# Three query projections normalised in their exponentials, and the first four weight blocks loaded by pairs of input channels

## Chip, cores and metric

One core of one Trainium2 chip runs the kernel. The metric is the device time of one execution in microseconds; 1082.49 is the median of three runs of the kernel before. TensorE (PE in the profile) multiplies, VectorE (DVE) and ScalarE (ACT) do the elementwise work, GpSimd (POOL) a little of it, and SyncE (SP) issues most of the loads.

## The reference, cut to what matters

One decoder layer over 256 tokens of width 1024: a convolution branch and sparse attention share one input projection, then comes attention over a memory of 256 tokens, then a layer of 16,384 experts chosen by product keys (PEER).

```python
def rmsnorm(x, g):
    xf = x.astype(jnp.float32)
    y = xf * lax.rsqrt(jnp.mean(xf * xf, axis=-1, keepdims=True) + EPS)
    return (y * g.astype(jnp.float32)).astype(x.dtype)
...
        hn = rmsnorm(h, mix_norm_g[l])
        proj = hn @ w_in[l]
        conv_a, conv_b, q, k_c, v_c, k_s, v_s, k_w, v_w, gate_logits = jnp.split(proj, IN_SPLITS, axis=-1)
        y_conv = conformer_conv(conv_a, conv_b, conv_dw_w[l], conv_dw_b[l], conv_ln_g[l], conv_ln_b[l])
        y_nsa = nsa_mixer(q, k_c, v_c, k_s, v_s, k_w, v_w, gate_logits, positions,
                          cmp_pos[l], cmp_w1[l], cmp_b1[l], cmp_w2[l], cmp_b2[l])
        h = h + jnp.concatenate([y_conv, y_nsa], axis=-1) @ w_out[l]
        h = h + memory_attention(rmsnorm(h, mem_q_norm_g[l]), rmsnorm(mem, mem_kv_norm_g[l]),
                                 w_mem_q[l], w_mem_k[l], w_mem_v[l], w_mem_o[l])
        h = h + peer(rmsnorm(h, peer_norm_g[l]), peer_w_q[l], peer_sub_keys[l], peer_u[l], peer_v[l])
    return rmsnorm(h, final_norm_g)
```

The norm's factor is one number per token, so it can be multiplied in behind a projection. Where the projection gives queries, the factor scales a whole row of scores, and a positive factor changes neither the row's order nor the place of its maximum.

## The kernel before

All activations lie transposed: 128 channels on the partitions, 256 tokens along the free axis, 8 chunks of channels. A weight block is 128 x 1024 floats (512 KB). `wload` (line 124) brings one into one of four buffers named `raw`, from SP's queue. The input projection multiplies it as it is, eight matmuls of 256 columns into one accumulator (`proj1`, line 160). Later projections split it into a rounded part `hi` (ScalarE, line 141) and a remainder `lo` (VectorE, line 142; GpSimd for some), with three matmuls per chunk (`mm3`, lines 152 to 154).

TensorE's instructions run in the order in which the program writes them. On the other engines a scheduler sets the order when the kernel is built; each engine then works through its own list from first to last, so an instruction that waits holds up all behind it on its engine.

`Rstd` (line 197) makes the norm factors. `add` sums squares (`sa_`). `sums` (line 214) adds over the partitions with two tiny matmuls (`ss_`), and a chain of 12 small VectorE operations makes the factor per token as a column (`rsc_`, `.col`) and then two diagonal matrices (`dg_`). `rows` (line 229) spreads them with two matmuls (`sr_`) into a row over the tokens (`rs_`, `.row`), which ScalarE copies. The tags are x (the layer's input, `r0`), m (memory), c (convolution's norm, `rc`) and h, h2 (`r1`, `r2`; both print as h).

The program's course. TensorE begins with 14 passes over ones (`warm`, line 245). Lines 246 to 254 issue the first loads. `hx` is x times the gain. The loop at line 312 takes the convolution's eight weight blocks in pairs `pb`, `pa`: one block after the other, `r0.sums` behind the third, `r0.rows` in the middle of the fourth. `conv_in` (line 300) makes the gated input `u`, and 124 taps (line 298, `yc<-u`) follow on VectorE, handed out by `conv(n)` between other work and finished by `ln_mean` (sums `lsum`, lines 607 to 610) ahead of TensorE's `pmu` (line 616). Then come two blocks for keys and values, the rope's queries and keys (`pq`, in `qraw`), and the values. The memory's input `mT` (four loads of 256 KB) becomes `mg` and `mg_l`, and while the attention's chains run, TensorE is filled with the memory's keys and values (`pmk`, `pmv`). `scores` (line 548) takes 16 units: matmuls `pss`, maximum `amx`, exponential `ape`, sum `asm`. In `mq_out` (line 723) the memory's queries are multiplied with `r1.row` and split; `m_scores` follows. In the expert stage `pq_out` (line 829) multiplies with `r2.row`, `key_scores` (line 834) makes `psq`, copied out as `sco`, two blocks behind the projection. Then 16 rounds of top-k on VectorE choose experts while TensorE goes through the expert weights (`pu`, `Y`).

Of the kernel before, what the change touches and what calls it, by code (L numbers as in the profile page):

```python
# [89 lines left out]
def rope_constants():  # L90

    d = np.arange(P) % 64
    inv = (np.float32(500000.0) ** (-(np.arange(8, dtype=np.float32) * np.float32(2.0) / np.float32(16.0)))).astype(np.float32)
    return np.stack([np.where(d < 16, inv[d % 8], 0.0), np.where(d < 8, -1.0, np.where(d < 16, 1.0, 0.0))], axis=1).astype(np.float32)


def build(tc, A, out, dbg=None):
# [163 lines left out]


    posf = wk.tile([P, T], F32, name="posf", tag="tb")
    V.tensor_copy(posf, posi)
    ang = St = ch.tile([P, T], F32, name="St")
    V.tensor_scalar(ang, posf, Pm("inv"), None, op0=ALU.mult)
    kk = wk.tile([P, T], F32, name="kk", tag="ta")
    MAGIC = 12582912.0
    V.tensor_scalar(kk, ang, 1.0 / (2.0 * math.pi), MAGIC, op0=ALU.mult, op1=ALU.add)
    V.tensor_scalar(kk, kk, MAGIC, None, op0=ALU.subtract)  # L270
    c1 = 6.28125
    c2 = float((np.array([2.0 * math.pi - c1], np.float32).view(np.uint32) & np.uint32(0xFFFFF000)).view(np.float32)[0])
    c3 = 2.0 * math.pi - c1 - c2
    for c in (c1, c2, c3):
        V.scalar_tensor_tensor(ang, kk, -c, ang, op0=ALU.mult, op1=ALU.add)
    PIF = 3.1415925
    V.tensor_scalar(ang, ang, PIF, -PIF, op0=ALU.min, op1=ALU.max)
    aabs = Ct = ch.tile([P, T], F32, name="Ct")
    V.scalar_tensor_tensor(aabs, ang, -1.0, ang, op0=ALU.mult, op1=ALU.max)
    halfpi = cst.tile([P, 1], F32, name="halfpi")  # L280
    V.memset(halfpi, math.pi / 2)
# [29 lines left out]
    pend = []  # L311
    for i in range(4):
        pb = psum(T, f"pb{i}")
        wb = wload(A["w_in_t"][2 * i]) if i else w0
        proj1(pb, wb, hx)
        if i == 1:
            r0.sums()
        wa = wload(A["w_in_t"][2 * i + 1])
# [3 lines left out]
        proj1(pa, wa, hx, range(4))
        if i == 1:
            r0.rows()
            conv_in(*pend)
# [845 lines left out]
```

## Time and profile before

| | |
|---|---|
| median of three runs | 1082.49 us (1081.4 to 1082.73) |
| profiled execution, its own time | 1082.72 us |
| its span on the core | 1080.9 us |
| mean granted TensorE clock | 0.996 of full speed |
| TensorE busy | 1061.2 us, 98% |
| VectorE busy | 871.8 us, 81% |
| ScalarE busy | 580.0 us, 54% |
| GpSimd busy | 102.3 us, 9% |

Busy shares are means over the whole span. A wait counts only where TensorE, or a chain that it depends on, stands still for it. The profiled execution lies 0.23 us over the median.

### The profile page before, as it was taken

How to read it: one execution, taken by the hardware profiler on the slowest of the kernel's cores; microseconds unless marked ns; L12 is line 12 of the kernel's file. 1: busy time of each engine (PE TensorE's matmuls, PEld its weight loads, DVE VectorE, ACT ScalarE, POOL GpSimd, SP SyncE). 2: the span in 40 equal slices, each digit the busy share in tenths (PEclk: the TensorE clock that was granted, in tenths of full speed). 3: DMA queues.
4: the chain of work that ended last, by engine and by line, in shares of the span. 5: the costliest groups of instructions: out<-in, count | busy, mean ns of one | idle time of the engine just before them, and what ended most of it. 6: DMA issues, size and time to landing. Idle time of an engine off the chain costs nothing.

```text
span 1080.9 us, 20534 instructions
## 1 busy us (share of the span) xinstructions
PE 1061.2 (98%) x7346; PEld 976.3 (90%) x7346; DVE 871.8 (81%) x2226; ACT 580.0 (54%) x1334; POOL 102.3 (9%) x82
## 2 busy tenths in 40 slices
...
GB/s 245 247 127 151 98 99 117 196 98 174 159 116 178 178 193 167 160 162 157 162 164 163 163 150 160 156 203 201 194 190 193 194 192 192 195 194 193 195 195 78
DMA packets 51685, 182.45 MB, mean 169 GB/s; under 512 B 5760, under 2 KB 6528, under 8 KB 51456
## 3 DMA queue, kind: packets, MB, share of 16 engines
...
q14 instruction: 43, 0.35, 0.1%
HBM read 179.81 MB, written 1.05 MB: 167 GB/s over the span
## 4 chain that ended last, share of the span: by engine, by line
PE 85%; DVE 13%; ACT 1%; DMA 1%; issue 0%; SPq 0%; DVEq 0%; ACTq 0%
PE Y L1071 32%; PE pu L152 9%; PE pu L154 8%; PE pu L153 8%; PE pq L163 2%; PE pw L1017 1%; PE ppq L152 1%; PE ppq L153 1%; PE ppq L154 1%; PE pb L163 1%; PE pw L1018 1%; PE pa L163 1%; DVE ohx L948 1%; PE pmk L152 1%; DVE lo L142 1%; DVE ohx L946 1%
## 5 line engine op out<-in xcount | busy, mean ns | idle before, releaser
L141 ACT ACTIVATE hi<-raw 128x512 fp32r<-128x512 f32 x624 | 376.7, 626 | 176.7 <-PE pu L153 66.9
L142 DVE TENSOR_TENSOR lo<-raw,hi 128x512 fp32r<-128x512 f32 x556 | 369.1, 687 | 26.8 <-ACT hi L141 21.0
L152 PE MATMUL pu<-hn_h,hi 128*128 128x256 f32 x1024 | 296.3, 289 | 0.0
L154 PE MATMUL pu<-hn_h,lo 128*128 128x256 f32 x1024 | 290.7, 284 | 1.9 <-DVE lo L142 1.9
L153 PE MATMUL pu<-hn_l,hi 128*128 128x256 f32 x1024 | 290.7, 284 | 0.0
L154 PEld LDWEIGHTS pu<-hn_h,lo 128*128 128x128 f32 x1024 | 197.3, 193 | 2.1 <-DVE lo L142 2.1
L153 PEld LDWEIGHTS pu<-hn_l,hi 128*128 128x128 f32 x1024 | 197.4, 193 | 0.0
L152 PEld LDWEIGHTS pu<-hn_h,hi 128*128 128x128 f32 x1024 | 197.2, 193 | 0.0
L1071 PE MATMUL Y<-hi,al 128*128 128x512 f32 x512 | 158.3, 389 | 0.0
L1071 PE MATMUL Y<-lo,ah 128*128 128x512 f32 x512 | 158.3, 389 | 0.0
L1071 PE MATMUL Y<-hi,ah 128*128 128x512 f32 x512 | 158.2, 389 | 0.0
L1071 PEld LDWEIGHTS Y<-hi,al 128*128 128x128 f32 x512 | 96.1, 188 | 20.0
L1071 PEld LDWEIGHTS Y<-lo,ah 128*128 128x128 f32 x512 | 96.1, 188 | 19.9
L1071 PEld LDWEIGHTS Y<-hi,ah 128*128 128x128 f32 x512 | 96.1, 188 | 19.8
L167 DVE TENSOR_TENSOR al<-slB,ah 128x256 fp32r<-128x256 f32 x88 | 37.4, 425 | 86.1 <-PE Y L1071 86.1
L166 ACT ACTIVATE ah<-slB 128x256 fp32r<-128x256 f32 x88 | 36.8, 418 | 110.7 <-PE Y L1071 110.7
L142 POOL TENSOR_TENSOR lo<-raw,hi 128x512 fp32r<-128x512 f32 x68 | 94.8, 1421 | 11.8 <-ACT hi L141 9.2
L1023 ACT ACTIVATE slB<-pw 128x348 f32<-128x348 f32 (+31 forms) x64 | 32.5, 507 | 70.2 <-DVE slB L1022 57.0
L298 DVE SCALAR_TENSOR_TENSOR yc<-u,par,yc 128x256 f32<-128x256 f32 x120 | 54.8, 474 | 0.1
L167 DVE TENSOR_TENSOR al<-slA,ah 128x256 fp32r<-128x256 f32 x40 | 17.1, 428 | 37.3 <-PE Y L1071 37.3
L166 ACT ACTIVATE ah<-slA 128x256 fp32r<-128x256 f32 x40 | 16.7, 418 | 49.3 <-PE Y L1071 48.0
L152 PE MATMUL ppq<-gx_h,hi 128*128 128x256 f32 x128 | 37.4, 292 | 0.0
...
## 6 DMA issues: line engine op xcount, KB each, us to landing
raw<-u SPq DMA_DIRECT2D x128, 512.0 KB, 3.4
raw<-v SPq DMA_DIRECT2D x128, 512.0 KB, 3.3
...
```

The source lines that it names most:

```text
L141: S.activation(hi, r, AF.Copy)
L142: (engs or (V, V))[q].tensor_sub(lo, r, hi.bitcast(F32))
L152: PE.matmul(ps, w[0], xh, start=start, stop=False)
L153: PE.matmul(ps, w[0], xl, start=False, stop=False)
L154: PE.matmul(ps, w[1], xh, start=False, stop=stop)
L163: PE.matmul(ps, w[0][:, k * P:(k + 1) * P], x[:, k], start=k == 0, stop=k == KC - 1)
L166: S.activation(dst[0], src, AF.Copy)
L167: V.tensor_sub(dst[1], src, dst[0].bitcast(F32))
L298: V.scalar_tensor_tensor(yc[:, i], u[:, i, j:j + T], w, yc[:, i], op0=ALU.mult, op1=ALU.add)
L946: V.tensor_tensor(o4, o4, tif[:, side].unsqueeze(2).to_broadcast([P, 16, 16, 8]), op=ALU.mult)
L1023: S.activation(slB[:, done - J:, n0:n0 + 4].rearrange("p i n -> p n i"), pw[:, :, done:], AF.Copy, scale=1.0 / GSC)
L1071: PE.matmul(Y[nh][c], lhs[:, sl], wc[c][t], start=False, stop=i == KEYS - 1 and lhs is a[1], skip_group_check=True)
```

## The change

Three parts. First, the start: the first four weight blocks come as 16 loads of 128 KB, by pairs of input channels, each quarter of all four blocks behind the other, on SP's queue; x and the first 32 columns of the parameters are issued from ScalarE's queue. TensorE works on all four blocks side by side, channel by channel. `r0.sums` stands behind all four, `r0.rows` behind the fifth block. The constants of the rope and the angles' operations come after the projections instead of ahead of them. Second, `qraw`, the memory's queries and the experts' queries are taken out of PSUM without the norm's factor, and the exponentials scale by the factor's column (`r8`, `r16`, `r2c`). `r1` makes no row and no diagonals any more. Third, the key scores follow one block behind the projection instead of two.

```diff
-        if cnt[0] == 1:
-            nc.sync.dma_start(raw[:, 0:512], src[:, 0:512])
-            nc.sync.dma_start(raw[:, 512:], src[:, 512:])
-        else:
-            nc.sync.dma_start(raw[:, 0:n], src)
+        nc.sync.dma_start(raw[:, 0:n], src)
...
-        def sums(self):
+        def sums(self, rows=True):
...
             rsqrt(y, m, t, sh)
+            if not rows:
+                return
...
-    nc.sync.dma_start(xT[:, 0:2], A["xT"][:, 0:2])
-    nc.sync.dma_start(par, A["par"])
-    w0 = wload(A["w_in_t"][0])
-    posi = wk.tile([P, T], I32, name="posi", tag="rt")
-    nc.sync.dma_start(posi, A["pos"].partition_broadcast(P))
-    for q in range(1, 4):
-        nc.sync.dma_start(xT[:, 2 * q:2 * q + 2], A["xT"][:, 2 * q:2 * q + 2])
+    nc.scalar.dma_start(par[:, 0:32], A["par"][:, 0:32])
+
+    first = [[wts.tile([P, 512], F32, name=f"wf{c}{h}", tag=("hi", "lo")[c // 2], bufs=6) for h in range(2)] for c in range(4)]
+    for q in range(4):
+        nc.scalar.dma_start(xT[:, 2 * q:2 * q + 2], A["xT"][:, 2 * q:2 * q + 2])
+        for c in range(4):
+            o = 256 * (q % 2)
+            nc.sync.dma_start(first[c][q // 2][:, o:o + 256], A["w_in_t"][c][:, 256 * q:256 * q + 256])
+    nc.sync.dma_start(con1, A["con"][:, 0:NCON1])
+    nc.sync.dma_start(par[:, 32:], A["par"][:, 32:])
...
+    acc = [psum(T, f"p{'ba'[c % 2]}{c // 2}", "mm" if c > 1 else "at") for c in range(4)]
+    for k in range(KC):
+        for c in range(4):
+            PE.matmul(acc[c], first[c][k // 4][:, (k % 4) * P:(k % 4 + 1) * P], hx[:, k], start=k == 0, stop=k == KC - 1)
+    r0.sums()
+    for i in range(2, 4):
+        pb = psum(T, f"pb{i}")
+        proj1(pb, wload(A["w_in_t"][2 * i]), hx)
+        if i == 2:
+            r0.rows()
+            conv_in(0, acc[0], acc[1])
+            conv_in(1, acc[2], acc[3])
+            conv(6)
+        pa = psum(T, f"pa{i}")
+        proj1(pa, wload(A["w_in_t"][2 * i + 1]), hx)
+        conv_in(i, pb, pa)
+        conv(6)
+    nc.sync.dma_start(con2, A["con"][:, NCON1:])
+    posi = wk.tile([P, T], I32, name="posi", tag="rt")
+    nc.sync.dma_start(posi, A["pos"].partition_broadcast(P))
...
-        V.tensor_mul(dst, ps, r0.row)
+        if i < 2:
+            V.tensor_mul(dst, ps, r0.row)
+        else:
+            S.activation(dst, ps, AF.Copy)
...
+    V.tensor_scalar(r8, r0.col, 0.125, None, op0=ALU.mult)
+    V.tensor_scalar(r8n, r0.col, -0.125, None, op0=ALU.mult)
...
-        V.tensor_scalar(mx, mx, -0.125, None, op0=ALU.mult)
+        V.tensor_scalar(mx, mx, r8n[:, hf:hf + 1], None, op0=ALU.mult)
...
-            S.activation(pe[:, b, 0:W], ps[:, b], AF.Exp, scale=0.125, bias=mx[:, b:b + 1], accum_out=sm[:, b:b + 1])
+            S.activation(pe[:, b, 0:W], ps[:, b], AF.Exp, scale=r8[:, hf:hf + 1], bias=mx[:, b:b + 1], accum_out=sm[:, b:b + 1])
...
-        t = twk.tile([P, T], F32, name=f"mqt{i}", tag="mqt", bufs=4)
-        V.tensor_mul(t, ps, r1.row)
-        S.activation(mq_h[:, i], t, AF.Copy)
-        V.tensor_sub(mq_l[:, i], t, mq_h[:, i].bitcast(F32))
+        split((mq_h[:, i], mq_l[:, i]), ps)
...
-    pq0 = mq_chunk(0)
-    r1.sums()
-    pq1 = mq_chunk(1)
-    pq2 = mq_chunk(2)
-    r1.rows()
-    mq_out(0, pq0)
-    mq_out(1, pq1)
-    mq_out(2, pq2)
-    for i in range(3, KC):
+    for i in range(KC):
         mq_out(i, mq_chunk(i))
+        if i == 1:
+            r1.sums(rows=False)
+            for j in range(2):
+                V.tensor_scalar(r16[j], r1.col, (0.0625, -0.0625)[j], None, op0=ALU.mult)
...
-        V.tensor_mul(qt, ps, r2.row)
+        S.activation(qt, ps, AF.Copy)
...
-        todo.append((i, ps))
-        if i == 0:
+        todo.append((i, pq_out(i, ps)))
+        if i == 1:
             r2.sums()
-        if i < 2:
-            continue
-        if i == 2:
+            V.tensor_copy(r2c, r2.col)
+        if i == 3:
             r2.rows()
-            todo = [(j, pq_out(j, p)) for j, p in todo]
-            continue
-        todo[-1] = (i, pq_out(i, ps))
-        key_scores(*todo.pop(0))
-        if i == 3:
+        if i:
             key_scores(*todo.pop(0))
...
-            tc.keep_in_program_order(S.activation(ge, ge, AF.Exp))
+            tc.keep_in_program_order(S.activation(ge, ge, AF.Exp, scale=r2c[:, hf:hf + 1]))
```

The change also moves rows on the other engines, which the diff does not show. VectorE at the end of the first norm's chain in the kernel before (`rsc_x` the factor, `dg_x` its diagonals, `mg_l` the remainders of the memory's input, `tb` and `ta` the gated convolution's input):

```order
L195 SCALAR_TENSOR_TENSOR rsc_x<-t_x,rsc_x 128x2
L227 TENSOR_SCALAR dg_x<-con_63,rsc_x 128x128 x2
L419 TENSOR_SCALAR chalf<-rsc_x 128x2
L239 SCALAR_TENSOR_TENSOR mg_l<-mT,par,mg 128x256 x2
L302 TENSOR_TENSOR tb_236<-pb_169,rs_x 128x256
L306 SCALAR_TENSOR_TENSOR ta_240<-pa_181,rs_x 128x256
```

And VectorE at the same place in the changed kernel:

```order
L233 SCALAR_TENSOR_TENSOR mg_l<-mT,par,mg 128x256
L185 TENSOR_TENSOR t_x<-rsc_x 128x2
L186 TENSOR_TENSOR t_x<-t_x,m_x 128x2
L233 SCALAR_TENSOR_TENSOR mg_l<-mT,par,mg 128x256
L187 SCALAR_TENSOR_TENSOR rsc_x<-t_x,rsc_x 128x2
L203 TENSOR_TENSOR sa_m<-sa_m,sq_m_414 128x256
L221 TENSOR_SCALAR dg_x<-con_63,rsc_x 128x128 x2
```

Two of the memory's remainders and one addition of its squares (`sa_m`) moved ahead of `dg_x`.

VectorE ahead of the thirteenth score maximum (`amx300`, whose reduction is the next row behind these) in the kernel before; `lo341` is the second remainder of a block of the memory's values, `yc` are taps:

```order
L142 TENSOR_TENSOR lo341_1695<-raw34_1688,hi341_1694 128x512
L298 SCALAR_TENSOR_TENSOR yc_168<-u_166,par_64,yc_168 128x256
L566 TENSOR_TENSOR asm210_1508<-asm210_1508,gate_652 128x2
L298 SCALAR_TENSOR_TENSOR yc_168<-u_166,par_64,yc_168 128x256
L167 TENSOR_TENSOR nsa_l_873<-po1_1540,nsa_h_872 128x256
L298 SCALAR_TENSOR_TENSOR yc_168<-u_166,par_64,yc_168 128x256
L559 TENSOR_REDUCE amx211_1569<-pss211_1563 128x2
L298 SCALAR_TENSOR_TENSOR yc_168<-u_166,par_64,yc_168 128x256
L560 TENSOR_SCALAR amx211_1569<-amx211_1569 128x2
L142 TENSOR_TENSOR lo350_1803<-raw35_1800,hi350_1802 128x512
L298 SCALAR_TENSOR_TENSOR yc_168<-u_166,par_64,yc_168 128x256 x2
L565 RECIPROCAL asm211_1573<-asm211_1573 128x2
```

VectorE from the thirteenth maximum in the changed kernel, where the same remainder is called `lo291`:

```order
L561 TENSOR_REDUCE amx300_1633<-pss300_1627 128x2
L274 SCALAR_TENSOR_TENSOR yc_174<-u_172,par_64,yc_174 128x256
L568 TENSOR_TENSOR asm211_1594<-asm211_1594,gate_669 128x2
L562 TENSOR_SCALAR amx300_1633<-amx300_1633,r81_673 128x2
L274 SCALAR_TENSOR_TENSOR yc_174<-u_172,par_64,yc_174 128x256
L573 TENSOR_SCALAR ape211_1593<-ape211_1593,asm211_1594 128x256
L274 SCALAR_TENSOR_TENSOR yc_174<-u_172,par_64,yc_174 128x256
L573 TENSOR_SCALAR ape211_1593<-ape211_1593,asm211_1594 128x256
L274 SCALAR_TENSOR_TENSOR yc_174<-u_172,par_64,yc_174 128x256
L567 RECIPROCAL asm300_1637<-asm300_1637 128x2
L134 TENSOR_TENSOR lo291_1655<-raw29_1648,hi291_1654 128x512
```

The remainder moved from ahead of that maximum to ten rows behind it, with four taps and two scaled exponentials between.

VectorE ahead of the convolution's sums in the kernel before (`lsum` is ready with the last row but one):

```order
L560 TENSOR_SCALAR amx301_1668<-amx301_1668 128x2
L142 TENSOR_TENSOR lo360_1867<-raw36_1864,hi360_1866 128x512
L609 TENSOR_TENSOR lsum2_1659<-yc_168 128x256
L142 TENSOR_TENSOR lo361_1871<-raw36_1864,hi361_1870 128x512
L610 TENSOR_TENSOR lsum_1657<-lsum_1657,lsum2_1659 128x256
L565 RECIPROCAL asm301_1672<-asm301_1672 128x2
```

And in the changed kernel, up to the row that completes `lsum`:

```order
L562 TENSOR_SCALAR amx301_1689<-amx301_1689,r81_673 128x2
L274 SCALAR_TENSOR_TENSOR yc_174<-u_172,par_64,yc_174 128x256
L134 TENSOR_TENSOR lo301_1716<-raw30_1709,hi301_1715 128x512
L274 SCALAR_TENSOR_TENSOR yc_174<-u_172,par_64,yc_174 128x256
L567 RECIPROCAL asm301_1693<-asm301_1693 128x2
L134 TENSOR_TENSOR lo310_1824<-raw31_1821,hi310_1823 128x512
L274 SCALAR_TENSOR_TENSOR yc_174<-u_172,par_64,yc_174 128x256
L568 TENSOR_TENSOR asm301_1693<-asm301_1693,gate_669 128x2
L134 TENSOR_TENSOR lo311_1828<-raw31_1821,hi311_1827 128x512
L611 TENSOR_TENSOR lsum2_1680<-yc_174 128x256
L573 TENSOR_SCALAR ape301_1692<-ape301_1692,asm301_1693 128x256
L612 TENSOR_TENSOR lsum_1678<-lsum_1678,lsum2_1680 128x256
```

Taps stand there up to four rows ahead of `lsum2`, and three remainders, a reciprocal and a scaled exponential are in the stretch, where two remainders were. Counted from the thirteenth maximum to the last sum, both rows included, there are 5 taps in the kernel before and 11 in the changed one.

## Rows read from the trace of the kernel before

**Rows 1.** Part 4 of the page: the chain that ended last, by engine.
```profile
PE 85%; DVE 13%; ACT 1%; DMA 1%; issue 0%; SPq 0%; DVEq 0%; ACTq 0%
```
**Rows 2.** Timeline, TensorE, first 31 us: start, length, instruction, idle before it and releaser.
```profile
1.03 6.03 PE L245 MATMUL warm<-ones 128*128 128x128 f32 x28 [1.03 <-DVE ones L242]
...
10.00 4.53 PE L163 MATMUL pb<-hx,raw 128*128 128x256 f32 x12 [2.07 <-DVE hx L259]
...
21.27 0.50 PE L218 MATMUL ss_x<-ones,sa_x 128*128 128x1 f32 x4
...
24.51 0.71 PE L233 MATMUL sr_x<-dg_x,ones 128*128 128x128 f32 x4 [0.90 <-DVE dg_x L227]
...
26.79 3.62 PE L163 MATMUL pb<-hx,raw 128*128 128x256 f32 x16
...
30.24 3.62 PE L163 MATMUL pa<-hx,raw 128*128 128x256 f32 x16
```
**Rows 3.** Waits of TensorE over the span: total us, times, longest us.
```profile
PE sr_c L233 <- DVE dg_c L227: 2.3, 1, 2.3
...
PE pu L154 <- DVE lo L142: 1.9, 1, 1.9
...
PE sr_h L233 <- DVE dg_h L227: 1.4, 1, 1.4
...
PE pmu L616 <- DVE asm L565: 1.1, 1, 1.1
```
**Rows 4.** Stretches: length, busy time by engine, granted clock, DMA share, GB/s.
```profile
core 0: us, PE busy (x) PEld busy (x) DVE busy (x) ACT busy (x) POOL busy (x), PEclk, DMA share, GB/s
...
2.00:13.00 11.00, 8.93 (x37) 7.94 (x36) 5.36 (x20) 3.31 (x9) 0.82 (x6) 0.86 0.94 304
...
3.20:3.80 0.60, 0.60 (x5) 0.60 (x5) 0.00 (x0) 0.03 (x1) 0.00 (x0) 1.00 0.82 233
...
10.00:13.00 3.00, 3.00 (x7) 2.47 (x8) 3.00 (x11) 2.16 (x6) 0.00 (x0) 0.50 1.03 412
...
79.00:152.00 73.00, 72.56 (x556) 64.29 (x555) 63.17 (x198) 46.27 (x142) 0.00 (x0) 1.00 0.37 120
...
205.00:207.50 2.50, 1.15 (x10) 0.94 (x8) 2.26 (x12) 0.94 (x2) 0.00 (x0) 1.00 0.78 265
...
419.80:423.00 3.20, 3.20 (x17) 3.20 (x17) 3.10 (x9) 0.63 (x1) 0.00 (x0) 0.50 0.48 164
```
**Rows 5.** Timeline, VectorE, around the diagonals of the first norm.
```profile
24.17 0.48 DVE L227 TENSOR_SCALAR dg_x<-con,rsc_x 128x128 f32<-128x128 f32 x2
...
24.64 0.88 DVE L239 SCALAR_TENSOR_TENSOR mg_l<-mT,par,mg 128x256 fp32r<-128x256 f32 x2
```
**Rows 6.** Timeline, TensorE, last use of a weight remainder before the scores.
```profile
147.54 0.28 PE L454 MATMUL pmv<-lo,mg 128*128 128x256 f32 x1
```
**Rows 7.** Timeline, VectorE, from the thirteenth score maximum to the last sum.
```profile
146.13 0.42 DVE L559 TENSOR_REDUCE amx<-pss 128x2 f32<-128x256 f32 x1
...
147.01 0.48 DVE L298 SCALAR_TENSOR_TENSOR yc<-u,par,yc 128x256 f32<-128x256 f32 x1
...
147.41 0.61 DVE L571 TENSOR_SCALAR ape<-ape,asm 128x256 f32<-128x256 f32 x2
...
151.46 0.68 DVE L142 TENSOR_TENSOR lo<-raw,hi 128x512 fp32r<-128x512 f32 x1
...
152.06 0.42 DVE L610 TENSOR_TENSOR lsum<-lsum,lsum 128x256 f32<-128x256 f32 x1
```
**Rows 8.** Timeline, ACT and TensorE, end of the expert queries.
```profile
312.25 1.50 PE L840 MATMUL psq<-skp,pqt 128*128 128x128 f32 x12
...
312.33 0.63 ACT L141 ACTIVATE hi<-raw 128x512 fp32r<-128x512 f32 x1 [0.81 <-PE ppq L153]
...
313.56 1.09 ACT L843 ACTIVATE sco<-psq 128x512 f32<-128x512 f32 x2
...
314.21 0.38 PE L880 MATMUL Y<-zero 128*128 128x512 bf16 x1 [0.46 <-ACT sco L843]
```

More of the change, by code (lines that the diff above doesn't have):

```diff
@@ L36 @@
                   ("conv_b", 4), ("ln_g", 4), ("ln_b", 4), ("cmp_b1", 2), ("cmp_b2k", 1),
-                  ("cmp_b2v", 64), ("cmp_pos", 32), ("inv", 1), ("sgn", 1)):
+                  ("cmp_b2v", 64), ("cmp_pos", 32)):
     PC[_name] = (_n, _n + _w)
@@ L85, in constants @@
     put("rsel", rs.reshape(P, 512))
+    inv = (np.float32(500000.0) ** (-(np.arange(8, dtype=np.float32) * np.float32(2.0) / np.float32(16.0)))).astype(np.float32)
+    put("inv", np.where(d < 16, inv[d % 8], 0.0)[:, None])
+    put("sgn", np.where(d < 8, -1.0, np.where(d < 16, 1.0, 0.0))[:, None])
     put("iota16", np.broadcast_to(cc[None, :], (P, 16)))
     return c
[L90 to L94, printed above, removed]
 def build(tc, A, out, dbg=None):
@@ L260, in build @@
         r0.add(xT[:, k])
[L263 to L281, printed above, removed]
     u = ch.tile([P, 4, 30 + T], F32, name="u")
@@ L309, in conv_in @@
             taps.append(lambda j=j: tap(i, j))
-    pend = []
-    for i in range(4):
-        pb = psum(T, f"pb{i}")
[L314 to L318, printed above, removed]
-        if i == 0:
-            nc.sync.dma_start(con1, A["con"][:, 0:NCON1])
-        pa = psum(T, f"pa{i}")
[L322 to L325, printed above, removed]
-        proj1(pa, wa, hx, range(4, KC))
-        if i == 0:
-            pend = (i, pb, pa)
-        else:
-            conv_in(i, pb, pa)
+    acc = [psum(T, f"p{'ba'[c % 2]}{c // 2}", "mm" if c > 1 else "at") for c in range(4)]
@@ L331, in build @@
         conv(6)
     nc.sync.dma_start(con2, A["con"][:, NCON1:])
-    S.activation(St, ang, AF.Sin, scale=Pm("sgn"))
-    S.activation(Ct, aabs, AF.Sin, scale=-1.0, bias=halfpi)
+    posi = wk.tile([P, T], I32, name="posi", tag="rt")
+    nc.sync.dma_start(posi, A["pos"].partition_broadcast(P))
+    Ct = ch.tile([P, T], F32, name="Ct")
+    St = ch.tile([P, T], F32, name="St")
+    posf = wk.tile([P, T], F32, name="posf", tag="tb")
+    V.tensor_copy(posf, posi)
+    ang = wk.tile([P, T], F32, name="ang", tag="th")
@@ new lines, in build @@
+    V.tensor_scalar(ang, posf, C("inv"), None, op0=ALU.mult)
+    kk = wk.tile([P, T], F32, name="kk", tag="ta")
+    MAGIC = 12582912.0
+    V.tensor_scalar(kk, ang, 1.0 / (2.0 * math.pi), MAGIC, op0=ALU.mult, op1=ALU.add)
+    V.tensor_scalar(kk, kk, MAGIC, None, op0=ALU.subtract)
+    c1 = 6.28125
+    c2 = float((np.array([2.0 * math.pi - c1], np.float32).view(np.uint32) & np.uint32(0xFFFFF000)).view(np.float32)[0])
+    c3 = 2.0 * math.pi - c1 - c2
+    for c in (c1, c2, c3):
+        V.scalar_tensor_tensor(ang, kk, -c, ang, op0=ALU.mult, op1=ALU.add)
@@ L335, in build @@
+    PIF = 3.1415925
+    V.tensor_scalar(ang, ang, PIF, -PIF, op0=ALU.min, op1=ALU.max)
+    halfpi = cst.tile([P, 1], F32, name="halfpi")
+    V.memset(halfpi, math.pi / 2)
+    S.activation(St, ang, AF.Sin, scale=C("sgn"))
+    V.scalar_tensor_tensor(kk, ang, -1.0, ang, op0=ALU.mult, op1=ALU.max)
+    S.activation(Ct, kk, AF.Sin, scale=-1.0, bias=halfpi)
     S.activation(halfpi, Ct[:, 0:1], AF.Tanh)
@@ L419, in build @@
     V.tensor_scalar(chalf, r0.col, 0.5, None, op0=ALU.mult)
+    r8, r8n = [ch.tile([P, 2], F32, name=f"r8{j}") for j in range(2)]
+    V.tensor_scalar(r8, r0.col, 0.125, None, op0=ALU.mult)
+    V.tensor_scalar(r8n, r0.col, -0.125, None, op0=ALU.mult)
     for hf in range(2):
```

13 lines of the change are left out of this document (7 added, 6 removed).

## Prediction

> **What bounds the kernel now.** The chain of waits comes first [rows 1]: 85% of the span is TensorE and 13% VectorE. So a time changes where TensorE stands still, or where a short VectorE chain feeds it, and work taken off ScalarE or VectorE elsewhere is worth nothing by itself. The timeline of the first 31 us [rows 2] shows what there is to gain at the start: the warm-up ends at 7.06, the first block of weights stops 2.07 us for the scaled input, `sr_x` waits another 0.90, and the fifth block (`pb2`) begins at 26.79, the sixth (`pa2`) at 30.24; a block of eight matmuls is 3.45 us. The list of TensorE's waits [rows 3] gives the places behind it that the change touches: `sr_h` 1.4, `pmu` 1.1; `sr_c` 2.3 and `pu` 1.9 it leaves alone. The stretches [rows 4] give the rates of the loads, the granted clock after a stall, and VectorE's room: in 79 to 152 it works 63.17 of 73 us, so 9.8 us are free.
>
> **Start, bytes.** Four blocks now need 4 x 3.45 = 13.8 us from 7.06, so TensorE would be done with them at 20.86 and with `ss_x` (0.37, from 21.27 to 21.64 in rows 2) and `pb2` at 24.7. Then `sr_x` must come, and it waits for `dg_x`. In the kernel before it came 3.24 us after `ss_x` (21.27 to 24.51). Now two remainders of the memory's gain (`mg_l`, 0.44 each [rows 5]) and an addition of like size (`sa_m`) stand in VectorE's chain ahead of `dg_x`, about 1.2 us: 20.86 + 3.24 + 1.2 = 25.3 at the soonest. And these three wait for the first quarter of the memory's input, which stands on SP behind 16 pieces of weights (2,048 KB), 136 KB of constants, the parameters, four blocks (2,048 KB), 417 KB of constants, the positions (128 KB) and w2 (96 KB), while x (1,024 KB) shares the same time from ACT's queue: with itself 6.44 MB. In the kernel before 2 to 13 us ran at 304 GB/s on the mean [rows 4]. By that the last byte comes 21.2 us after 2.0, at 23.2; a landing some 0.8 later makes 24.0. Four ScalarE operations and the addition on it add about 2.55 (four at about 0.45, then 0.4, and the first diagonal with its handover 0.35): `sr_x` at 26.55. Behind `sr_x` and its 0.55 stands `pa2`, which is then at 27.1 where it was at 30.24: **-3.1**. Bounds: with all bytes at 412 GB/s [rows 4] they land at 18.4 and the 25.3 decides, -4.4; with all at the 233 GB/s of the stretch in which 1 KB rows moved [rows 4] they land at 30.4, `sr_x` comes at 33.0, and the start costs 3.3. I take the mean rate, since the stream ahead mixes 1 KB rows and 4 KB rows as that stretch did. The stop of 2.07 in front of the first block goes, as `hx` is made ahead of all else on VectorE.
>
> The Trainium skill, "DMA: Bandwidth & Descriptors", Rules for kernel authors and Bandwidth, speaks against this part: spreading loads over SP and ACT gives no bandwidth, and loads should be batched to 1 MiB, with 64 KB at 138 GB/s in its table. By 138 GB/s for the 3.2 MB in front, against the mean of 304, the landing would come 12.7 us later and the sum be about 1097. The trace does not agree with so low a rate, since the 134 KB of parameters moved with their neighbours at 233 GB/s [rows 4].
>
> VectorE's first tap moves too, as `rs_x` on ScalarE stands behind five gains and three squares of later quarters: to about 28 from 26. The rope's angles add 8 operations (3 us), four `qraw` products leave (1.6 us). All of that lies within the 9.8 us free before 152, less the 3.1 that TensorE is early; it costs nothing as long as that holds.
>
> **Attention, the taps.** The order puts about 5 us of taps later, behind the thirteenth maximum (`amx300`). In the kernel before five taps stood between it and the last sum, and 152.06 + 0.42 is 6.35 after 146.13 [rows 7]. Now there are 11 taps at 0.40 (4.4), 5 `lo` at 0.60 (3.0), three exponentials' factors at 0.27 (0.8), three sums at 0.34 (1.1), the reductions 0.34 and 0.60 (the wide one like an `lo` of its size), and seven small ones (0.5): 10.7, of which overlaps may take 0.2: 10.5. That is +4.2 on the time at which `pmu` can start. TensorE meets it in two places: it uses `lo291` at the matmul that stood at 147.54 [rows 6], 1.4 after `amx300`, but four taps, two factors, the reduce and three small ones are ahead of it (2.7) and it takes 0.67 itself, so TensorE stops about 2.0 there, and the rest of the 10.5, some 3.2, at `pmu`, where 1.1 stood [rows 3]: 2.0 + 3.2 - 1.1 = **+4.1**. Bounds 3.6 (the `lo` on time and all small ones overlapped) and 4.7 (no overlap). Both ends hang on `amx300` itself, which TensorE's scores release and which comes as early as TensorE does, so the 3.1 of the start is not lost twice.
>
> **Clock.** After the stop of 1.91 us before `lo` at 419 the granted clock was 0.50 for 3.2 us, and after the 2.07 at 10 us for 3; after the 1.35 at 207 it was 1.00, though TensorE worked 1.15 of 2.5 us [rows 2 to 4]. Two stops of 2.0 and 3.2 within 6 us lie nearer to the first: I take 3.2 us at half rate, **+1.6**; the other end is 0.
>
> **Memory queries.** The two `sr_h` matmuls (0.47) and the wait of 1.4 for `dg_h` go [rows 3]. In their place an `lo` of the third block comes later, as VectorE splits `pmq` at once; about 0.2 stays: **-1.6**. Bounds -0.4 (the `lo` late by 1.4 instead) and -1.9. Its eight products leave VectorE, but there TensorE is what is waited for.
>
> **Expert queries.** The key scores follow one block behind instead of two, so one pair of them (a third of the 1.50 for three pairs, 0.5 [rows 8]) now lies ahead of the last block. After it the last query is copied by ScalarE, behind an `hi` of 0.63 that starts as the block ends, and only then come the last pair and the two `sco` of 0.54. From 314.21 the first `Y` goes to as much as 315.1. If the `hi` finds its buffer sooner the copy does too, and nothing is lost. Between 0 and +0.9 I take **+0.6**, nearer the row, since that `hi` was released by the last block. The 16 products that VectorE loses (6.6 us) are in a stretch that ends with VectorE waiting for TensorE; the new column copy and the scaled exponents are tiny.
>
> **Sum.** -3.1 + 4.1 + 1.6 - 1.6 + 0.6 = +1.6 on the profiled 1082.72, which lies 0.2 over the median of the runs: 1084.3. A measurement of this kernel tells about 0.2% (2.2 us) from no change, so this counts as the same.
>
> **Rivals.** 1. *No half clock* after the two stops: 1082.7. For it the 1.35 at 207, against it 419. 2. *The loads in front are slow*: 16 pieces at 233 GB/s and whatever stands behind late, the price +3.3 in place of -3.1, so 1090.7; with half of that, 1087.5. It decides from a landing of the memory's first quarter after 27 us (then the start gives nothing), and it ends slower. For it the 233 of 1 KB rows; against it the 304 of the mean and that TensorE uses a quarter (0.77 MB) in 3.45 us, 223 GB/s. 3. *Faster*: VectorE has less to do in the expert queries, its top-k chain ends earlier, and the 1.9 wait at `pu` goes together with the half clock behind it: -3.5, giving 1080.8, and with no half clock in the attention or fast loads (-1.3) 1079.2 to 1079.5. Against it, VectorE already waits for the last block there. 4. *The stops in the attention don't come*, VectorE having run ahead through its 9.8 us: -4.1 -1.6, 1078.6. Against it, the order on that engine is fixed, and the taps stand behind a maximum that TensorE releases. The change does what it says in each; no step of it can fall away.
>
> The Trainium skill, "TensorE: Matmul & The Clock Gate", What's actually happening, has the clock halved after an idle array; by it the first rival would be out, and the sum stays 1084.3. The stop at 207 does not agree, that at 419 does.
>
> **Numbers.** Forecast 0.40, rival 1 0.24, rival 2 0.16, rival 3 0.10, rival 4 0.10. Loads between the two rates move each by up to 1.3 down and 6.4 up. Over 1084.7 lie 0.4 of the forecast's chance, 0.07 of rival 1's share and all of rival 2: 0.34. Under 1080.3 lie most of rivals 3 and 4 and 0.05 of the forecast and rival 1: 0.22. The rest, 0.44, is the same. The range from 1078.8 to 1088.8 leaves out the slow half of rival 2 and half of rival 4.
>
> **To be seen.** Right: `pb` from 7.06 without a stop, `sr_x` at 25 to 28 with `dg_x` as releaser behind the memory's gains; a stop near 2 us at `pmv` for `lo` and one near 3 at `pmu`; no `sr_h` of the memory queries; `Y` late by under 1 us. Wrong: `sr_x` beyond 30 (loads), stops at `pmu` no longer than 1.1 (the taps), a granted clock of 1.00 after them, or the wait at `pu` gone.

## The result, and the profile after

The changed kernel takes 1096.78 us (median of 4 runs, 1095.65 to 1100.09) against 1081.95 for the kernel before, beside which it ran: ratio 1.0144 [1.0118, 1.017]. It is 1.4% slower, clear of the spread of the runs, and outside the range. The profiled execution is the longest of the four, 1100.09 us with a span of 1098.2 (before 1082.72 and 1080.9), so the rows below hold 3.3 us that the median run doesn't have. The mean granted clock is 0.989 (before 0.996).

The chain of waits reads as in [rows 1], 85% TensorE and 12% VectorE, so the question is again where TensorE stands still or works more slowly. The first matmul of each stage tells where the time came in:

| place on TensorE | before, us | after, us | late by | this step predicted | measured |
|---|---|---|---|---|---|
| `pkv`, behind the convolution's blocks | 40.6 | 41.3 | 0.7 | -3.1 | +0.7 |
| `pmu`, end of the attention | 152.6 | 157.5 | 4.9 | +4.1 | +4.2 |
| `sr_c`, the layer norm of the convolution | 168.1 | 175.5 | 7.4 | +1.6 (clock) | +2.5 (clock) |
| `pmq`, memory queries | 196.3 | 204.6 | 8.3 | | +0.9 (clock) |
| `pms`, memory scores | 213.8 | 220.0 | 6.2 | -1.6 | -2.1 |
| `pu`, expert keys done | 318.6 | 324.9 | 6.3 | +0.6 | +0.1 |
| first `Y` of the last stage | 724.8 | 731.7 | 6.9 | | +0.6 |
| last `Y` | 1072.8 | 1089.8 | 17.0 | | **+10.1** |

The largest row belongs to no step of the prediction. The last stage, 1536 matmuls `Y` in three groups of 512, takes 358.1 us from first to last start in place of 348.0: 233 ns each in place of 226.6. The groups of instructions by tile show it on all of them (durations in ns: least, median, most; then the first and last start). The kernel before:

```profile
L1071 PE MATMUL Y<-hi,ah x512: 388/389/397, 724.8 to 1072.3; 128*128 128x512 f32 x171
L1071 PE MATMUL Y<-hi,al x512: 388/389/393, 725.8 to 1072.8; 128*128 128x512 f32 x171
```

The changed kernel:

```profile
L1064 PE MATMUL Y<-hi,ah x512: 395/396/397, 731.7 to 1089.4; 128*128 128x512 f32 x171
L1064 PE MATMUL Y<-hi,al x512: 392/396/397, 732.6 to 1089.8; 128*128 128x512 f32 x171
```

Not a few of them are slow: the medians rise by 7 ns, and so does that of the third group (`Y<-lo,ah`, 389 to 396). No wait shows, the clock is 1.00, and the diff has no line there.

The list of TensorE's waits after (total, times, longest, us), for [rows 3]:

```profile
PE pmu L618 <- DVE lsum L612: 3.5, 1, 3.5
PE sr_x L227 <- DVE dg_x L221: 3.0, 1, 3.0
PE pu L146 <- DVE lo L134: 2.6, 1, 2.6
PE sr_c L227 <- DVE dg_c L221: 2.3, 1, 2.3
PE pmv L456 <- DVE lo L134: 2.0, 1, 2.0
...
PE psq L838 <- ACT pqt L829: 0.4, 1, 0.4
```

`pmv` 2.0 and `pmu` 3.5 are the two stops of the attention, near the 2.0 and 3.2 foretold; `sr_h` is gone; `sr_x` waits 3.0. TensorE's timeline at the start (start, length), for [rows 2]:

```profile
20.49 0.50 PE L210 MATMUL ss_x<-ones,sa_x 128*128 128x1 f32 x4
20.85 3.70 PE L155 MATMUL pb<-hx,raw 128*128 128x256 f32 x16
27.54 1.20 PE L227 MATMUL sr_x<-dg_x,ones 128*128 128x128 f32 x4 [2.99 <-DVE dg_x L221]
28.52 6.04 PE L155 MATMUL pa<-hx,raw 128*128 128x256 f32 x16
34.40 3.62 PE L155 MATMUL pb<-hx,raw 128*128 128x256 f32 x16
```

The four blocks end where foretold (20.49 for 20.86). `sr_x` starts at 27.54 for 26.55, and the next block takes 6.04 us where it took 3.62 [rows 2]. Two loads stand in VectorE's chain ahead of `sr_x`: a cast of a constant waits for the second part of the constants, and the memory's first remainder waits for its gain, which starts on ScalarE when the memory's input lands (VectorE's and ScalarE's timelines):

```profile
22.76 0.23 DVE L544 CAST causb<-con 128x128 bf16<-128x128 f32 x1 [7.01 <-DMA con<-con]
25.05 0.51 ACT L232 ACTIVATE mg<-mT,par 128x256 fp32r<-128x256 f32 x1 [11.91 <-DMA mT<-memT]
25.60 0.48 DVE L233 SCALAR_TENSOR_TENSOR mg_l<-mT,par,mg 128x256 fp32r<-128x256 f32 x1 [0.96 <-ACT mg L232]
```

The stretches of the changed kernel, for [rows 4]:

```profile
core 0: us, PE busy (x) PEld busy (x) DVE busy (x) ACT busy (x) POOL busy (x), PEclk, DMA share, GB/s
2.00:10.00 8.00, 8.00 (x42) 7.61 (x41) 2.22 (x8) 2.31 (x4) 0.58 (x5) 1.00 0.99 316
28.50:34.00 5.50, 5.50 (x17) 4.43 (x16) 4.17 (x12) 3.21 (x9) 0.00 (x0) 0.55 0.33 131
157.50:163.00 5.50, 5.50 (x22) 4.62 (x23) 4.95 (x14) 3.00 (x9) 0.00 (x0) 0.50 0.56 188
177.00:181.00 4.00, 4.00 (x24) 4.00 (x23) 3.74 (x13) 3.36 (x11) 0.00 (x0) 0.60 0.00 0
```

The loads of the first 8 us ran at 316 GB/s, with 128 KB pieces. Behind each of the three long stops (`sr_x`, `pmu`, `sr_c`) the granted clock stands at about half for 4 to 5.5 us: the level of 1.2 GHz where it was 2.4.

### The profile page after: what moved, and what is told of

Read it like the earlier page. It is cut to its first block, busy times and chain, and to the rows that moved or that the text cites. A ratio compares the mean times of both kernels' runs of the same rounds, so it can differ in the third digit from the quotient of the medians.

```text
span 1098.2 us, 20543 instructions
## 1 busy us (share of the span) xinstructions
PE 1074.3 (98%) x7342; PEld 978.6 (89%) x7342; DVE 864.4 (79%) x2201; ACT 587.6 (54%) x1353; POOL 101.4 (9%) x82
## 4 chain that ended last, share of the span: by engine, by line
PE 85%; DVE 12%; DMA 2%; ACT 1%; issue 0%; SPq 0%; ACTq 0%; DVEq 0%
PE Y L1064 32%; PE pu L144 9%; PE pu L146 8%; PE pu L145 8%; PE pq L155 2%; PE pw L1010 1%; PE ppq L145 1%; PE ppq L144 1%; PE ppq L146 1%; PE pw L1011 1%; DVE ohx L941 1%; DMA mT<-memT 1%; PE pa L155 1%; PE pmk L144 1%; DMA xT<-xT 1%; PE pmw L145 1%
## 5 line engine op out<-in xcount | busy, mean ns | idle before, releaser
L1064 PE MATMUL Y<-hi,ah 128*128 128x512 f32 x512 | 161.8, 396 | 0.0
L1064 PE MATMUL Y<-lo,ah 128*128 128x512 f32 x512 | 161.8, 396 | 0.0
L1064 PE MATMUL Y<-hi,al 128*128 128x512 f32 x512 | 161.8, 396 | 0.0
```

What stands on the lines that cost most here:

```text
L1064: PE.matmul(Y[nh][c], lhs[:, sl], wc[c][t], start=False, stop=i == KEYS - 1 and lhs is a[1], skip_group_check=True)
```

## The experiments

Ratios are to the kernel before, run beside each on the same chip, with 95% intervals. **Why `Y` is slower:** the change has one small new tile, `r2c`, two columns in a pool; by the program's allocation, everything that is allocated behind it moves by 32 bytes on each partition. `Y` holds `ah` and `al` and streams `hi` and `lo`. `hi` began at 36,128 and begins at 19,744, `ah` began at 130,848 and begins at 130,880. My theory was that the address counts. The rivals: the weight buffers' new place, or the changed timing ahead of the stage.

**`a1`**, the changed kernel with `r2c` in spare columns of a constant, which puts `ah` back:

```diff
-    halfpi = cst.tile([P, 1], F32, name="halfpi")
+    halfpi3 = cst.tile([P, 3], F32, name="halfpi")
+    halfpi, r2c = halfpi3[:, 0:1], halfpi3[:, 1:3]
...
-    r2c = tk.tile([P, 2], F32, name="r2c")
```

> The changed kernel with its new column r2c placed in spare columns of another constant tile, so that everything allocated behind it, the expert activations' parts ah and al (TensorE's stationary operand in the last stage) among them, goes back by 32 bytes to its old address; nothing else differs. Theory shift (the 32 bytes slow the last stage, where one matmul of 512 columns went from 226.6 to 233.1 ns): 226.6 ns again, 10 us less than the changed kernel, about 1087. Theory weights (the new place of the weight buffers does it): still 233 ns, time unchanged at about 1096 to 1097. Theory state (a slower chip, no address): still 233 ns and the kernel before just as slow beside it.

Measured: 1089.35 us, 1.0055 [1.0038, 1.0072]. `Y` is as quick as before:

```profile
L1064 PE MATMUL Y<-hi,ah x512: 388/389/397, 732.5 to 1080.0; 128*128 128x512 f32 x171
```

So 0.9% of the 1.44% came from `r2c`'s place alone.

**`a2`**, the changed kernel with the weight buffers allocated in the old order (`+ wts.tile([P, 1024], F32, name="raw0", tag="raw", bufs=4)` ahead of the first blocks).

> The changed kernel with the buffers raw, hi and lo allocated in their old order, so that the weight buffers lie where they lay before; the 32-byte shift behind r2c stays. Theory weights: 226.6 ns per matmul in the last stage, about 1087. Theory shift: still 233 ns, 1096 to 1097.

Measured: 1095.31, 1.0112 [1.0086, 1.0137]; `Y` from 726.5 to 1084.7, 358.2. The weight buffers' place isn't it.

**`b1`**, the kernel before with nothing but a pad (`+ pad = tk.tile([P, 2], F32, name="pad")`, set to zero), and **`b2`**, the kernel before with its `hi` and `lo` allocated ahead of `raw`.

> The kernel before with 32 bytes of padding where the change put r2c, so that ah and al move by 32 bytes; nothing else. Theory shift: 233 ns per matmul in the last stage and 10 us more, about 1092. Theory weights: 226.6 ns and no change, 1082.

> The kernel before with hi and lo allocated ahead of raw, as the change does: the rounded parts and remainders move down by 16 KB, raw up by 24 KB. Theory weights: 233 ns and 10 us more, about 1092. Theory shift: 226.6 ns and no change, 1082.

Measured: `b1` 1091.83, 1.0087 [1.0067, 1.0108], `Y` 358.2 long; `b2` 1083.0, 1.0001 [0.9992, 1.0011], `Y` 348.0. `Y` in `b1`:

```profile
L1074 PE MATMUL Y<-hi,ah x512: 395/396/397, 721.9 to 1079.6; 128*128 128x512 f32 x171
```

An unused tile of 8 bytes per partition costs the kernel before nine microseconds. Since nothing but places and one memset differs in `b1`, the timing ahead of the stage is out as a cause; `b7` and `b8` below have the same memset and are quick. Which step of the address matters was then asked with other sizes of the pad: 16 columns (**`b3`**, 64 bytes), 32 (**`b6`**, 128), 64 (**`b7`**, 256), 128 (**`b8`**, 512); with a pad between `ah` and `al` (**`b4`**); and with 32 bytes ahead of `raw`, `hi`, `lo`, `ah` and `al` alike (**`b5`**):

```diff
+    cpad = cst.tile([P, 8], F32, name="cpad")
+    G.memset(cpad, 0.0)
```

> The kernel before with 64 bytes of padding where 32 bytes cost 6.6 ns per matmul of the last stage. Theory parity (the operand's address counts modulo 64: 32 over is quick, 0 over is slow): 226.6 ns again, the time of before, 1083. Rival (any shift from the old place is slow, or the address counts by a larger step): 233 ns and some 10 us more, 1092.

> The kernel before with 32 bytes of padding between ah and al, so that al alone moves, and nothing else on TensorE's path. Theory stationary (the slow part is the operand that TensorE holds, and only where it is the shifted one): the matmuls of al slow, those of ah quick, a third of the 10 us, about 1086. Rival (something else that stood behind r2c was the cause): all three kinds at 226.6 ns, 1083. Third way: all three kinds slow alike, because the two alternate.

> The kernel before with 32 bytes of padding ahead of the weight buffers, so that raw, hi, lo and ah, al all move by 32 bytes: their distances stay, their own places change. Theory relative (quick where held and streamed operand have the same address modulo some step of 128 to 512 bytes, as in the kernel before, 288 modulo 512 both): 226.6 ns per matmul of the last stage, 1083. Theory absolute (the place of ah and al alone counts): 233 ns, 1091 to 1092.

> The kernel before with 128 bytes of padding where r2c stands, so that ah and al move by 128 bytes and the weight buffers don't. Theory step 128: 226.6 ns again and 1083. Theory larger step (256 or 512), or any shift slow: 233 ns and 1090 to 1092.

> The kernel before with 256 bytes of padding where r2c stands; ah and al move by 256 bytes against hi and lo. Step 256: 226.6 ns per matmul of the last stage, 1083. Step 512: 233 ns, 1090 to 1093.

> The kernel before with 512 bytes of padding there. Step 256 or 512: 226.6 ns, 1083. No step at all (only the old distance is quick): 233 ns, 1090 to 1093.

| kernel | `ah` moved against `hi`, bytes | ratio | `Y`, first to last start, us |
|---|---|---|---|
| `b1` | 32 | 1.0087 [1.0067, 1.0108] | 358.2 |
| `b3` | 64 | 1.0072 [1.0056, 1.0087] | 358.2 |
| `b6` | 128 | 1.008 [1.0061, 1.0099] | 356.7 |
| `b7` | 256 | 1.0007 [0.9996, 1.0018] | 347.9 |
| `b8` | 512 | 1.0008 [0.9999, 1.0018] | 347.9 |
| `b5` | 0, all moved by 32 | 0.9998 [0.9987, 1.0008] | 347.9 |
| `b4` | `al` alone by 32 | 1.0087 [1.0069, 1.0105] | 355.9 |

One row of each kind, `b7`, `b6`, `b5` and `b4`:

```profile
L1074 PE MATMUL Y<-hi,ah x512: 389/389/398, 724.9 to 1072.4; 128*128 128x512 f32 x171
```

```profile
L1074 PE MATMUL Y<-hi,ah x512: 390/393/404, 726.7 to 1082.9; 128*128 128x512 f32 x171
```

```profile
L1073 PE MATMUL Y<-hi,ah x512: 389/389/397, 724.2 to 1071.7; 128*128 128x512 f32 x171
```

```profile
L1072 PE MATMUL Y<-hi,ah x512: 387/395/398, 726.5 to 1081.9; 128*128 128x512 f32 x171
```

In all of these but `b4` the place of the held operand against the streamed one, modulo 256 bytes, tells quick from slow: both places of `hi` and the old one of `ah` leave 32, the new one of `ah` leaves 64. A first guess of 64 fell with `b3`, and in `b5`, where all moved by 32 together, nothing is slow. `b4` doesn't follow from that rule alone: the matmuls with `ah`, which hadn't moved, are slow too. Its expectation had this as a third way, as those with `ah` and `al` alternate; no run tells that from another cause, so it stays open.

**The start and the attention.** **`c1`** is the kernel before with the second and third part of the change (factors in the exponentials, `r2c` in the constant); **`c2`** is the kernel before with the new start alone.

> The kernel before with the second and third part of the change alone (factors in the exponentials, key scores one block behind), the start as it was, and r2c where it moves no address. VectorE's list then has 1 tap between the thirteenth maximum and the last sum instead of 5 before and 11 in the change. Theory start (the new start pushes the taps back and so makes the stops at pmv and pmu): no wait at pmv, none or under 0.3 at pmu, no sr_h wait in the memory queries, 2 to 3 us less than before, about 1080. Theory factors (the unscaled copies on ScalarE and the later column make the stops): waits of 2 and 3 us at pmv and pmu here too, 1085 or more.

> The kernel before with the first part of the change alone, the start with 16 pieces, four blocks side by side and the angles behind them. 10 taps stand between the thirteenth maximum and the last sum. Theory start: a wait of 2.5 to 3 us at sr_x with half clock behind it, 2.0 at pmv and about 2.5 at pmu with half clock behind them, 7 to 9 us more than before, 1089 to 1091. Theory factors: the waits at pmv and pmu stay away, and only sr_x and its half clock cost, less the earlier first block: 1082 to 1084.

Measured: `c1` 1081.51, 0.9976 [0.9962, 0.999]; `c2` 1089.41, 1.0054 [1.0042, 1.0066]. TensorE's waits in `c1`, where neither `pmv`, `pmu` nor `sr_h` is listed:

```profile
PE pb L163 <- DVE hx L261: 3.0, 1, 3.0
PE pu L154 <- DVE lo L142: 1.9, 1, 1.9
PE sr_c L235 <- DVE dg_c L229: 1.8, 1, 1.8
```

And in `c2`:

```profile
PE pmu L612 <- DVE lsum L606: 3.5, 1, 3.5
PE pmv L450 <- DVE lo L134: 2.5, 2, 1.4
...
PE sr_x L227 <- DVE dg_x L221: 2.1, 1, 2.1
```

The factors by themselves pay 0.24%. The new start is what puts the taps behind the thirteenth maximum: 10 in `c2`, 11 in the changed kernel, 5 before, 1 in `c1`. `c1` and `c2` add up to +0.30%, and both together in `a1` give +0.55%; VectorE's order comes out anew in each, but the gap is no wider than the intervals, so that the parts don't add up is not shown.

**`a3`** measures the clock's price: `a1` with seven throwaway matmuls in the wait ahead of `pmu`.

```diff
+        for _ in range(7):
+            PE.matmul(pmu, ones, hx[:, 0], start=True, stop=True)
```

> The changed kernel with r2c elsewhere (1089.35 in an earlier run) and seven matmuls of 256 columns, whose result is thrown away, ahead of pmu in the place where TensorE stands still for 3.3 us. VectorE's list is as it was. Theory clock: the granted clock stays at 1.00 behind pmu where it was 0.50 for some 6 us, 2 to 3 us less, 1086.5 to 1087.5. Rival (the half clock is not from that stop, or the matmuls are not enough): 0.50 behind pmu as before, and 1089 or more.

Measured: 1086.23, 1.0027 [1.0017, 1.0038], against 1.0055 for `a1`: 0.28%, or 3.0 us, with intervals that touch only at 1.0038. In the two traces it is 2.6 us between `pmu` and `sr_c`; `a3`'s also has no half clock behind `sr_x`, where `a1`'s has 0.72 in 27 to 33. The stretches, `a1` and then `a3`:

```profile
152.00:158.00 6.00, 2.66 (x16) 2.45 (x16) 4.83 (x15) 2.27 (x7) 0.00 (x0) 0.78 0.32 108
158.00:164.00 6.00, 6.00 (x27) 5.01 (x26) 4.82 (x14) 3.57 (x11) 0.00 (x0) 0.54 0.43 156
```

```profile
152.00:158.00 6.00, 6.00 (x34) 4.93 (x34) 4.92 (x15) 2.58 (x9) 0.00 (x0) 0.95 0.50 175
158.00:164.00 6.00, 6.00 (x43) 4.56 (x42) 4.58 (x13) 4.63 (x15) 0.00 (x0) 1.00 0.29 94
```

With work in the stop the clock stays at 1.00 behind it and TensorE starts 43 matmuls in place of 27 in the 6 us.

**`a4`** and **`a5`** ask whether the memory's input holds up the start. `a4` is `a1` with each load of it made to wait for `r0` (`+ G.tensor_copy(mT[:, 2 * q, 0:2], r0.col)` ahead of it); `a5` also issues `con2` right behind `con1`.

> The changed kernel with r2c elsewhere (1089.35), and the memory's four loads held back until the first norm's column is there, so that their gains and squares leave VectorE's and ScalarE's lists ahead of dg_x and rs_x. Theory (sr_x waits for the memory's first quarter): sr_x at 24.5 to 25 instead of 27, its wait under 1 and the granted clock at 1.00 behind it, 3 to 5 us less, 1084.5 to 1086.5; the stops of 2 and 3 at pmv and pmu stay, with 10 taps behind the maximum. Rival (the second part of the constants, or the chain itself, sets sr_x): the wait stays above 2, 1088 or more.

> The changed kernel with r2c elsewhere, the memory's loads held back (1088.5 together) and the second part of the constants loaded ahead of the next four weight blocks instead of behind them. Theory (both loads stood ahead of dg_x on VectorE): sr_x at 24 to 25, its wait under 1, the granted clock at 1.00 behind it, 2 to 4 us less, 1085 to 1086.5; the stops at pmv and pmu stay. Rival (something third holds the chain): the wait stays over 2 and the time at 1088.

Measured: `a4` 1088.47, 1.005 [1.0036, 1.0064]; `a5` 1088.79, 1.0051 [1.0038, 1.0065]. Neither came down to the 1086.5 expected at most. In `a4` the wait stayed, because another load stood in VectorE's list ahead of the chain. TensorE's and VectorE's timelines:

```profile
26.90 0.68 PE L227 MATMUL sr_x<-dg_x,ones 128*128 128x128 f32 x4 [3.05 <-DVE dg_x L221]
```

```profile
23.95 0.23 DVE L546 CAST causb<-con 128x128 bf16<-128x128 f32 x1 [7.45 <-DMA con<-con]
```

In the changed kernel the same cast had stood there and waited to 22.76, 2.3 us ahead of the memory. So two loads, not one, were in that chain. In `a5` both are gone, and `sr_x` starts at 24.87 without a wait; but TensorE's list of waits has:

```profile
PE pmv L458 <- DVE lo L134: 4.1, 2, 2.6
PE pmu L620 <- DVE lsum L614: 2.9, 1, 2.9
```

`pkv` now starts at 35.7, 4.9 us sooner than in the kernel before, and `pmu` still at 156.9 (before: 152.6). The gain is gone by `pmu`, with stops at `pmv` and `pmu`. But holding the memory back also changes VectorE's list, and that is what went with the loss: `a2`, whose VectorE list is the changed kernel's row for row, is as early at `pkv` as `a4` (37.9 and 37.8) and has its thirteenth maximum 4.6 us sooner. `a2`, then `a4`:

```profile
142.97 0.40 DVE L562 TENSOR_REDUCE amx<-pss 128x2 f32<-128x256 f32 x1
```

```profile
147.59 0.43 DVE L563 TENSOR_REDUCE amx<-pss 128x2 f32<-128x256 f32 x1 [0.44 <-PE pss L561]
```

In `a4` and `a5` TensorE has already stopped 2.6 us for a late remainder at `pmv` before that (until 130.11 in `a5`).

**`a6`** is `a5` with more taps let through ahead, so that none stands behind the thirteenth maximum (`conv(6)` to `conv(8)` in the attention's loop).

> The same with constants early, and the taps handed out eight instead of six at a time in the attention's loop; VectorE's list then has no tap and no remainder between the thirteenth maximum and the last sum. Theory (the stops at pmv and pmu are the pushed-back taps and nothing else): no wait at pmv and pmu and no half clock behind them, 7 to 9 us less than with constants early alone, 1076 to 1079. Rival (VectorE has too little time before, so that remainders come late sooner): waits for lo at pmk or pmv in their place, 1081 or more.

Measured: 1082.49, 0.9994 [0.9985, 1.0003]. That is 6.3 us under `a5`, so the taps' order cost at least that there, but it falls short of the 1076 to 1079 expected, and the rival came true. `pkv` at 34.6 is 6.0 us ahead of the kernel before, and `pmu` at 152.9 is not ahead at all. VectorE's room in 55 to 79, `a6`:

```profile
55.00:79.00 24.00, 24.00 (x131) 21.16 (x129) 24.00 (x69) 8.57 (x20) 0.00 (x0) 1.00 0.49 165
```

It has none there, 24.00 of 24 us, but the kernel before has next to none either, 23.76. TensorE later stops for remainders from VectorE, 3.4 us at `pmk` (114.21) and 1.2 at `pmv`.

**`d1`** is what the parts point to: `c1`, and the load of the positions moved behind those of x, since `c1`'s longest wait is for x.

```diff
-    posi = wk.tile([P, T], I32, name="posi", tag="rt")
-    nc.sync.dma_start(posi, A["pos"].partition_broadcast(P))
     for q in range(1, 4):
         nc.sync.dma_start(xT[:, 2 * q:2 * q + 2], A["xT"][:, 2 * q:2 * q + 2])
+    posi = wk.tile([P, T], I32, name="posi", tag="rt")
+    nc.sync.dma_start(posi, A["pos"].partition_broadcast(P))
```

> The factors alone, and in the old start one load moved: the positions (128 KB, broadcast) go behind the three quarters of x instead of ahead of them. Theory (the first block's wait of 2.1 for hx is x standing behind the positions): the wait under 0.5, the granted clock at 1.00 in 10 to 13 us where it was 0.50, 2 to 3.5 us less than the factors alone, about 1077. Rival (the weights or the parameters come as late): the wait moves to another releaser, and the time is that of the factors alone within 1 us.

**`d2`** is `d1` with ten throwaway matmuls in the wait ahead of `sr_c` (`+ PE.matmul(ps[:, 0:P], ones, ones, start=True, stop=True)`).

> The factors alone with the positions later (1077.8 in an earlier run), and ten small matmuls of 128 columns, thrown away, ahead of sr_c, where TensorE stands still for 2.3 us and the granted clock is 0.50 behind it for some 3 us. Theory clock: 1.00 behind sr_c, 1 to 2 us less, 1076 to 1077. Rival (the filling delays sr_c, or the clock falls all the same): no change or up to 0.5 more.

Measured: `d1` 1077.79, 0.9945 [0.9933, 0.9957]; `d2` 1077.29, 0.9944 [0.9931, 0.9958]. Both beat both kernels by half a per cent and more; the two can't be told apart. The start of `d1`, TensorE's timeline and then stretches, the second that of the layer norm:

```profile
9.01 1.13 PE L163 MATMUL pb<-hx,raw 128*128 128x256 f32 x4 [1.60 <-DVE hx L261]
```

```profile
10.00:13.00 3.00, 2.95 (x11) 1.62 (x11) 2.97 (x11) 2.38 (x5) 0.00 (x0) 1.00 1.03 410
164.00:172.00 8.00, 7.06 (x43) 6.60 (x44) 6.27 (x21) 4.88 (x14) 0.00 (x0) 0.79 0.12 46
```

The layer norm's in `d2`:

```profile
164.00:172.00 8.00, 7.99 (x63) 7.11 (x63) 6.42 (x19) 5.29 (x15) 0.00 (x0) 1.00 0.09 17
```

`d1` is 0.31% under `c1`, as expected, but not by the expected way. The stop at the start is 1.60 us, not under 0.5 (2.07 before, 3.0 in `c1`). The clock behind it is not halved as it was in [rows 4], but neither is `c1`'s, 1.00 in 10 to 13. At `pkv` the traces of `c1` and `d1` differ by 0.9 us (39.8 and 38.9); where the rest comes from is not shown. In `d2` the clock stays at 1.00 through the norm, without a gain in the time that the runs could show.

## Why the prediction was wrong

**The sum lacked its largest term.** The change part by part went through instructions, bytes and waits, and called the new column copy `r2c` tiny. Its time is, but the 32 bytes by which it moved `ah` and `al` were worth +10.1 us. Without them (`a1`) the change costs 0.55%, some 6 us, at the range's upper end (1088.8 is 0.58% over 1082.49): the other terms missed by about 4.4 more. That rest seems to come and go with the half clock: `a2`, with the same list on VectorE, costs 12.1 us with the bytes and so about 2.0 without, near the sum's 1.6. In their traces, one of four runs each, the half clock stands behind `sr_x`, `pmv`, `pmu` and `sr_c` in `a1`, and of these only behind `pmv` and `pmu` in `a2`.

**Start, bytes: -3.1 became +0.7.** The parts held nearly all: four blocks to 20.5, the memory's input as the releaser, landing 25.05 for 24.0, `sr_x` 1.0 late. Rival 2 was not it, since the landing came under its 27 and the loads ran at 316 GB/s. By the table in the Trainium skill, "DMA: Bandwidth & Descriptors", Bandwidth, which has 64 KB at 138 GB/s, the sum would have been 1097, an estimate; that figure comes near to the result by chance, as the traces do not agree with its rate. What failed is the clock: I charged none behind `sr_x`, whose matmuls then took 0.98 us for 0.55, and `pa2` took 2.4 us more than before. VectorE's cast that waits for the second constants, 2.3 us ahead of the memory, wasn't in the chain that I added up; in `a1` it came at 23.55 and the memory no longer made VectorE wait. In `a2` the clock stayed up, and `pkv` came at 37.9: -2.7 for -3.1. TensorE's timeline and stretch in `a2`:

```profile
26.98 0.68 PE L227 MATMUL sr_x<-dg_x,ones 128*128 128x128 f32 x4 [3.18 <-DVE dg_x L221]
```

```profile
27.00:33.00 6.00, 6.00 (x30) 5.35 (x31) 6.00 (x19) 3.94 (x12) 0.00 (x0) 1.00 0.72 249
```

**"The 3.1 of the start is not lost twice"** held where VectorE's list was the changed kernel's: in `a2` `pkv` was 2.7 us earlier than before and the thirteenth maximum 3.2 (142.97 for 146.13 [rows 7]); in `a1` both were 0.9 earlier. It didn't hold in `a4` to `a6`, where the memory's loads were held back: `pkv` was 2.8, 4.9 and 6.0 us early, and that maximum 1.5, 0.8 and 1.5 late. Whether the rows that moved on VectorE cost it, or an engine that is full from 55 to 79 in all of them, no run separates. That `a2`'s list kept the gain speaks against the second, as VectorE is as full there, 23.99 of 24.

**Attention, the taps: right in the profiled execution**, +4.2 for +4.1, with both stops where foretold; `a6` took the taps away and 6.3 us with them. From `pkv` to `pmu` `a2` and `a1` take 5.2 and 5.9 us more than the kernel before, with the clock at 0.59 and 0.73 in 148 to 152, behind the stop at `pmv`, where the changed kernel's profile has 1.00; that +4.2 comes so near is in part luck. Rival 4 is out.

**Clock: right mechanism, too small, and a matter of the execution.** +1.6 was taken; behind `pmu` the records give +2.5 and `a3` 3.0, and behind `sr_c`, which was left out as unchanged, another 0.9. Rival 1 is out for `pmu`. Behind `sr_x` the changed kernel, `a1` and `a2`, with one list on VectorE, stopped 2.99, 2.6 and 3.18 us, and the clock read 0.50, 0.72 and 1.00 in 27 to 33; the longest stop kept it. In `a4` too, a stop of 3.05 us had 1.00 behind it:

```profile
27.00:33.00 6.00, 6.00 (x30) 5.36 (x31) 5.13 (x18) 3.83 (x11) 0.14 (x1) 1.00 0.86 286
```

By the Trainium skill, "TensorE: Matmul & The Clock Gate", What's actually happening, the clock halves behind an idle window of a monitor that runs free of the kernel, so that its timing varies from run to run. The three stops at `sr_x` agree with that. A stop need not fill such a window, so the one at 207, which the prediction held against the rule, isn't against it.

**Memory queries: right**, -2.1 for -1.6. **Expert queries:** +0.1 for +0.6, within its bounds: `psq` waits 0.4 us for the copy, as foretold. **Rival 3** (the wait at `pu` goes) is out: 2.6 us after, 1.9 before.
